# A hybrid streaming encoder step: one more gate pair as products of halves, the attention's values left in two halves, inverse sums by pairs

## The chip, the cores and the metric

The kernel runs on one core of a Trainium2 chip. The metric is device time in microseconds (us) of one execution. It is measured in several runs, and their median counts. A profile of one execution by the hardware profiler gives busy times, waits and the order in time; its span is the time from the first to the last instruction that the profiler saw.

## What is computed

One layer of an encoder step for a prompt of 1024 frames and a batch entry of 64 new frames (`sample`, with a cache of 128), together T = 1088 rows, in float32. Cut to what matters:

```python
xn = rms_norm(x, g_pre)
z = xn @ w_in                       # 1024 -> 8208 columns
xa, ga, q, k, v, gb, fl, ma, mb = jnp.split(z, ...)
ua, conv_new = causal_conv(xa, conv_hist, conv_w, conv_b)
ya, h_new = rg_lru(ua, h0, ...)     # gated recurrence over time
ya = ya * jax.nn.silu(ga)
logf = jax.nn.log_sigmoid(fl + b_f)
yb = fox_prompt(q, k, v, logf)      # causal softmax attention, 16 heads of 64;
                                    # logits + cum(logf)[query] - cum(logf)[key]
yb = yb.reshape(B, L, W_B) * jax.nn.silu(gb)
u = jnp.einsum('bsnw,nwd->bsnd', jnp.stack([ya, yb], axis=2), w_branch)
gates = jax.nn.sigmoid(jnp.stack([ma, mb], axis=2))
mix = jnp.sum(gates * u, axis=2) @ w_o
h = x + rms_norm(mix, g_post)
ple = jax.nn.sigmoid(h @ w_ple_gate) * (pe @ w_ple_proj)
return h + rms_norm(ple, g_ple), (k, v, logf, h_new, conv_new)
```

## The kernel before, in words

Everything stands transposed: 128 channels on the partitions, the rows of x along the free axis. A float32 product is made of three matmuls of halves: each operand is split into a rounded high half (`xh`, `wh`, by a copy on ScalarE, `copy_act` L89) and the rest as the low half (`xl`, `wl`, a subtraction on VectorE, `sub` L92), and high x high, low x high and high x low are added in PSUM.

The stages in order of time are:

- 0 to 145 us: x is normalised and turned; the projections v and forget gates, and two plain gate panels.
- 145 to 433 us, **the quads**: k, q and some of the other projections are made as *products of halves* (`seven`, L899). Two panels of 128 columns and two halves of the inputs form a 2 x 2 product that is made of seven products of sums instead of eight. A pair of panels takes 7 x 24 = 168 matmuls of 272 columns in place of 144 of 364 or 360. VectorE, ScalarE and GpSimd form the sums and add up the results. There are 13 such pairs; `MORE = 3` (L37) of them are gate pairs taken from the back of the deque `gates`, whose last entries are those of C_GB, the gate of branch B.
- 433 to 845 us, **the attention**: 64 units (16 heads x 4 blocks `q2` of 256 queries), plus 8 steps for pairs of heads of the sample. A unit is made of steps on TensorE: logits `s` (`scores`, L1203), turning the powers `t` (`turn`, L1228), and the product with v (`values`, L1255). Between them TensorE works at **filler** steps: plain gate panels in steps of three matmuls (`filler`, L1097), which need nothing of the attention. A planner in the kernel's own code (L1447 to L1490) sets the order: it books times of each engine and takes an attention step when its inputs will have been ready for `MARGIN(ahead_by)` ns, else a filler step. `ahead_by` says how many filler steps were used up beyond an even share of the attention so far; the margin falls from 600 ns by 60 per step, to no less than −300 (L50). What filler is left runs behind the last attention step.
- 845 to 1043 us: branch A's convolution, gates and recurrence.
- 1043 to 1111 us, **the panels of branch A**: `ya` times its half of w_branch, times sigmoid of the gate ma, written to `d_mix` (`evac_a`, L1862, one GpSimd DMA for each chunk of 364 or 360 columns). At the same time the inputs of branch B are read back: `branch_in` (L1819) loads a row block k of `d_y` and `d_gb`, `branch_b` (L1830) multiplies it by silu(gb), and `branch_out` splits it into `ybh` and `ybl`. Row blocks 0 and 1 are early ones with rooms of their own (`EARLY`, L1847), and blocks 2 to 7 use two buffers `yb_in` in turn.
- 1111 to 1207 us: the panels of branch B; then the output product, the normalisations and the embedding.

In the attention, a unit's softmax (`softmax`, L1187) takes for each half `par` of its 256 queries: exponentials with their sum `sm` on ScalarE (L1191), the inverse of the sum on GpSimd (as a power of −1, L1193), and the scaling of the powers by it on GpSimd (L1194). The value product leaves a bank `pv` of 128 partitions, whose lower 64 hold the product with v's high half and the upper 64 that with its low half. ScalarE copies the upper half to `lo`, VectorE adds the lower half to it (`y`, 64 x 256, L1293), and GpSimd issues the DMA of y to `d_y` (L1297). The deque `v_free` has two rooms for `pv`; a room is free again when the addition is done (L1295).

Of the kernel before, what the change touches and what calls it, by code (L numbers as in the profile page):

```python
# [8 lines left out]
F32 = mybir.dt.float32  # L9
# [5 lines left out]
P = 128  # L15
# [18 lines left out]
CW = HT // 2  # L34
PLAIN = 2

MORE = 3  # L37
W_SC = 1092
GC = 364

HOP_PE, HOP = 250.0, 90.0
D_MAX, D_LO, D_Y, D_YS = (240.0, 1.035), (130.0, 1.1), 420.0, 230.0
A_EXP, A_HI, A_LO, A_ST, A_W = (450.0, 0.85), (150.0, 0.88), 380.0, 470.0, 1060.0
G_NORM, G_INV = (260.0, 0.84), 220.0
G_DMA = 860.0
D_W = 1240.0

# [4 lines left out]


AHEAD = 4000
WAKE = 36
GA_EARLY = (1, 3, 5)
LN1P = [1.0 / 15, 1.0 / 13, 1.0 / 11, 1.0 / 9, 1.0 / 7, 1.0 / 5, 1.0 / 3]
# [16 lines left out]
def hybrid_step(tc, a, o):  # L74
# [24 lines left out]
    d_cq = dram.tile([2, NH, DEC], F32, name="d_cq")  # L99
    d_ma = dram.tile([KT, P, T], F32, name="d_ma")  # L100
    d_mb = dram.tile([KT, P, T], F32, name="d_mb")
    d_y = dram.tile([NP, P, T], F32, name="d_y")
    d_gb = dram.tile([KT, P, T], F32, name="d_gb")
    d_ga = dram.tile([KT, P, T], F32, name="d_ga")
    d_x = [dram.tile([P, T], F32, name=f"d_x{k}") for k in range(2)]
# [950 lines left out]
    def per(cost, n):  # L1056
        return cost[0] + cost[1] * n
# [117 lines left out]
        at = book("G", smp_at[p], 490.0, lambda: pool.tensor_copy(vs[:, :, 0, :], v_smp[:, :, :]))  # L1175
        t["vs_at"] = book("G", at, 740.0, lambda: sub(pool, vs[:, :, 1, :], v_smp[:, :, :], f(vs[:, :, 0, :])))

    def tiny2(name):
        return p2.tile([P, 1], F32, name=name, tag=name, bufs=12 if name == "nm" else 8)[:, :]

    def lowest(s, w, out, m, least=-NEG):

# [1 line left out]
        return nm, book("D", now[0] + HOP_PE, per(D_MAX, w), lambda: dve.tensor_tensor_reduce(  # L1184
            out=out, in0=s[:, :w], in1=m, scale=-1.0, scalar=least, op0=ALU.add, op1=ALU.min, accum_out=nm))

    def softmax(at, nm, n, pr):  # L1187


        sm = tiny2("sm")  # L1190
        at = book("A", at, per(A_EXP, n), lambda: act.activation(  # L1191
            out=pr[:, :n], in_=pr[:, :n], func=AF.Exp, scale=-1.0, bias=nm, accum_out=sm))
        at = book("G", at, G_INV, lambda: pool.tensor_tensor(out=sm, in0=sm, in1=warm[:, :], op=ALU.pow))  # L1193
        return book("G", at, per(G_NORM, n), lambda: pool.tensor_scalar(  # L1194
            out=pr[:, :n], in0=pr[:, :n], scalar1=sm, scalar2=1.0, op0=ALU.mult, op1=ALU.mult))

    def width(q2, par):
        n = 256 * q2 + (par + 1) * P
# [4 lines left out]
    def scores(x, i, pr):  # L1203

        h, q2 = units[x]
        t = heads[h]
        half, par = divmod(i, 2)
        n, w = width(q2, par)
        q0 = (2 * q2 + par) * P
        c = slice(half * w, (half + 1) * w)  # L1210
        s = p2s.tile([P, 512], F32, name="s", tag="s")
        pe.matmul(s[:, :w], t["q1"][:, q0:q0 + P], t["k1"][:, c], start=True, stop=False)  # L1212
        pe.matmul(s[:, :w], t["q2"][:HD + 4, q0:q0 + P], t["k2"][:HD + 4, c], start=False, stop=True)  # L1213
        spent(logits_ns(w))
        nm, at = lowest(s, w, pr[:, c], mask[:, SEQ - n + c.start:SEQ - n + c.stop],
                        nm_first.pop((x, par)) if half else -NEG)
        if c.stop < n:
            nm_first[x, par] = nm
            return at, at
        return at, softmax(at, nm, n, pr)  # L1220

    turned, turned_by = {}, {}
    n_diag = [0]
# [27 lines left out]
        return book("D", at, per(D_LO, n), lambda: sub(dve, tl[:, :n], tp[:, :n], f(th[:, :n])))  # L1251

    pvs = {}
    lo_free = [0.0]
    def values(u, g, h, q2):  # L1255
        vv = heads_v[h]
        if g == 0:
            pvs[u] = pv_half()
        pv = pvs[u]
        th, tl = turned.pop((u, g))  # L1260
        high = turned_by.pop((u, g))
        def part(j, x, **kw):
            v = vv[:, 2 * g + j, :, :].rearrange("p s d -> p (s d)")
            if g < q2:
                return pe.matmul(pv[:, :256], v, x[:, j * 256:(j + 1) * 256], **kw)  # L1265
            c0 = P if j else 0
            return pe.matmul(pv[:, c0:256], v, x[:, :P] if j else x[:, P:3 * P], **kw)  # L1267

        def high_part(j, stop=False):
            tc.declare_no_dep(part(j, th, start=False, stop=stop).ins, high.ins, reason="ordered through the low part")  # L1270

        if g < q2:
            for j in range(2):
                part(j, tl, start=(g == 0 and j == 0), stop=False)
                high_part(j)
            spent(480.0)
            return
        if q2 == 0:
            part(0, tl, start=True, stop=False)
            part(1, tl, start=False, stop=False)  # L1280
            high_part(1)
        else:
            part(1, tl, start=False, stop=False)
            high_part(1)
            part(0, tl, start=False, stop=False)
        high_part(0, True)
        spent(460.0)
        lo = p2.tile([HD, 256], F32, name="lo", tag="lo", bufs=1)
        y = p2.tile([HD, 256], F32, name="y", tag="y", bufs=3)

        dst = d_y[h // 2][(h % 2) * HD:(h % 2 + 1) * HD, q2 * 256:(q2 + 1) * 256]
        at = book("A", max(now[0] + HOP_PE, lo_free[0]), A_LO, lambda: copy_act(lo[:, :], pv[HD:, :256]))
        at = book("D", at, D_Y, lambda: dve.tensor_tensor(out=y[:, :], in0=pv[:HD, :256], in1=lo[:, :], op=ALU.add))  # L1293
        v_free.popleft()
        v_free.append(at)  # L1295
        lo_free[0] = at
        book("G", at, G_DMA, lambda: pool.dma_start(dst, y[:, :]))  # L1297


# [10 lines left out]
    def sample_scores(p):  # L1310
# [3 lines left out]
        pe.matmul(s[:, :LS], cs_q[:, :], cs_k[:, :], start=False, stop=True)  # L1314
        spent(440.0)
        nm, at = lowest(s, LS, prs_s[:, :LS], mask_s[:, :])
        return at, softmax(at, nm, LS, prs_s)

    def sample_turn(p):
        t = smp[p]  # L1320
# [9 lines left out]
    def sample_values(p):  # L1330
        t = smp.pop(p)
        pv = pv_half()
        for i in range(2):
            pe.matmul(pv[:, :], t["vs"][:, i, 0, :], t["pt"][:, i, :, :].rearrange("p s n -> p (s n)"),
                      start=(i == 0), stop=False)
            pe.matmul(pv[:, :P], t["vs"][:, i, 1, :], t["pt"][:, i, 0, :], start=False, stop=(i == 1))
        spent(458.0)
        ys = p2.tile([P, DEC], F32, name="ys", tag="ys", bufs=1)
        ats = []
        for j in range(2):  # L1340
            js, ks = slice(j * HD, (j + 1) * HD), slice(P + j * HD, P + (j + 1) * HD)
            ats.append(book("A", now[0] + HOP_PE, per(A_HI, HD), lambda js=js, ks=ks: copy_act(ys[js, :], pv[js, ks])))
        for j, at in enumerate(ats):
            js = slice(j * HD, (j + 1) * HD)
            at = book("D", at, D_YS, lambda js=js: dve.tensor_tensor(out=ys[js, :], in0=pv[js, js], in1=ys[js, :],
                                                                     op=ALU.add))
        book("D", at, 0.0, lambda: sp.dma_start(d_y[p][:, SEQ:], ys[:, :]))
        v_free.popleft()
        v_free.append(at)

# [19 lines left out]
    due = {}  # L1372
    s_free = deque([0.0, 0.0, 0.0])
    t_free = deque([0.0, 0.0])
    v_free = deque([0.0, 0.0])
    prs = {}
    seen = {"t": 0, "v": 0}
    last_t = {u: ("t", u, q2) for u, (h, q2) in enumerate(units)}
# [62 lines left out]
            t_free.append(due[step])  # L1441
        done.add(step)

    pool.memset(warm[:, :], -1.0)
    booking = tc.manual_schedule(engines={act.engine, dve.engine, pool.engine})
    booking.__enter__()
    load_head(0)  # L1447
# [16 lines left out]
    own = 0.0  # L1464
    filled = 0
    n_fill = 3 * KT * (1 + sum(e[0][0] == "r" for e in ahead) + sum(len(g[1]) for g in gates))
    head_start = n_fill
    while s_q or t_q or v_q:
        catch_up()
        times = [(i, ready(q[0])) for i, q in enumerate((s_q, t_q, v_q)) if q]  # L1470
        times = [(i, at) for i, at in times if at is not None]
        ahead_by = filled - head_start - (n_fill - head_start) * own / own_total
        best = next((i for i, at in times if at + MARGIN(ahead_by) <= now[0]), None)
        if best is None:
            at, first_ = min((at, i) for i, at in times) if times else (now[0] + 1e9, None)
# [6 lines left out]
        step = (s_q, t_q, v_q)[best].popleft()  # L1482
        own += own_time(step)
        if step == ("v", 0, 0):
            head_start = filled - n_fill * own / own_total
        go(step)
    while next(fill, False):
        catch_up()
# [328 lines left out]
        return ybpool.tile([P, T], dt, name=name, tag=f"yb{i}{k}")  # L1817

    def branch_in(k, t, z):  # L1819
        sp.dma_start(t[:, :], d_y[k])  # L1820
        sp.dma_start(z[:, :], d_gb[k])
        return t, z

# [574 lines left out]
```

## Time and profile before

| | |
|---|---|
| median of three runs | 1430.43 us (1429.32 to 1431.48) |
| the profiled execution | 1429.49 us |
| its span in the profile | 1427.5 us |
| its granted TensorE clock | 0.998 |
| instructions, all engines | 25022 |
| bytes moved by DMA | 201.20 MB, mean 141 GB/s |

In the profile PE is TensorE (matmuls), PEld its weight loads, which overlap with them, DVE is VectorE, ACT is ScalarE, POOL is GpSimd and SP the engine that issues most DMAs; a q behind the name means its queue. A row of a group gives the line, the engine, the operation and its tiles with their shapes (out<-in), the count, busy time, mean ns of one, and the idle time before them with what ended it. A DMA has two times: that of its issue on the engine and that from the issue to the landing.

### The profile page before, as it was taken

The numbers are of one execution on the slowest core, as the hardware profiler recorded it, in microseconds if no ns is written. First come the engines' busy times: TensorE is split into PE (matmuls) and PEld (weight loads), VectorE is DVE, ScalarE is ACT, GpSimd is POOL, SyncE is SP. The second block draws the span as 40 slices with busy tenths as digits, with TensorE's granted clock in tenths as the row PEclk, the third lists the DMA queues.
The fourth block names the chain that finished last, engine by engine and source line by source line (L and its number), as shares of the span: only waits on it lengthen the run. The fifth ranks groups of instructions, "written<-read, shape, count | busy, mean of one in ns | idle before, by whom it ended". The sixth has DMA issues, their size and how long they took to land.

```text
span 1427.5 us, 25022 instructions
## 1 busy us (share of the span) xinstructions
PE 1410.8 (99%) x9217; PEld 1358.0 (95%) x9217; DVE 899.4 (63%) x1638; ACT 720.5 (50%) x1339; POOL 436.5 (31%) x652
## 2 busy tenths in 40 slices
PE   9999999999999999999999999999999999999997
PEld 8999999999999999999999999999999999888887
DVE  5564766564432666666666656898767474777654
ACT  5423544442222666666666657777544232565443
POOL 0012322233204777768776841221011000000001
PEclk9999999999999999999999999999999999999999
DMA  6667556765247764556566545564467774224211
GB/s 225 214 133 107 150 155 193 162 180 141 85 122 194 182 130 131 137 110 151 123 150 131 84 101 106 83 101 84 165 211 264 252 237 136 113 74 150 78 48 45
DMA packets 138919, 201.20 MB, mean 141 GB/s; under 512 B 24372, under 2 KB 98844, under 8 KB 137772
## 3 DMA queue, kind: packets, MB, share of 16 engines
q1 hardware_dynamic: 119436, 158.96, 44.2%
q0 software_dynamic: 8160, 23.25, 5.9%
q10 hardware_dynamic: 11200, 17.38, 3.4%
q8 instruction: 73, 1.20, 0.3%
q14 instruction: 50, 0.41, 0.1%
HBM read 131.60 MB, written 66.36 MB: 139 GB/s over the span
## 4 chain that ended last, share of the span: by engine, by line
PE 82%; DVE 6%; DMA 5%; ACT 3%; issue 3%; POOL 1%; SPq 0%; DVEq 0%; ACTq 0%; POOLq 0%
PE quad L844 17%; PE acc L179 11%; PE acc L181 11%; PE acc L180 11%; PE q L2042 5%; PE tp L1244 4%; PE pv L1265 3%; PE s L1213 2%; PE s L1212 2%; PE pv L1267 2%; PE vacc L179 1%; PE vacc L180 1%; PE vacc L181 1%; DMA w_raw<-in_w_in 1%; PE vacc L500 1%
## 5 line engine op out<-in xcount | busy, mean ns | idle before, releaser
L179 PE MATMUL acc<-xh,wh 128*128 128x364 f32 x720 | 237.6, 330 | 0.2 <-ACT st L90 0.2
L181 PE MATMUL acc<-xh,wl 128*128 128x364 f32 x720 | 235.8, 328 | 0.0
L180 PE MATMUL acc<-xl,wh 128*128 128x364 f32 x720 | 235.8, 327 | 0.0
L179 PEld LDWEIGHTS acc<-xh,wh 128*128 128x128 f32 x720 | 135.4, 188 | 1.2 <-ACT st L90 0.5
L180 PEld LDWEIGHTS acc<-xl,wh 128*128 128x128 f32 x720 | 135.3, 188 | 0.8
L181 PEld LDWEIGHTS acc<-xh,wl 128*128 128x128 f32 x720 | 135.1, 188 | 0.0
L90 ACT ACTIVATE wh<-w_raw 128x1024 fp32r<-128x1024 f32 (+1 forms) x66 | 63.4, 962 | 86.4 <-PE quad L844 34.4
L93 DVE TENSOR_TENSOR wl<-w_raw,wh 128x1024 fp32r<-128x1024 f32 (+1 forms) x55 | 62.5, 1138 | 67.6 <-ACT wh L90 47.0
L1193 POOL TENSOR_TENSOR sm<-sm,warm 128x1 f32<-128x1 f32 x136 | 79.2, 582 | 57.0 <-ACT pb L1191 21.8
L93 DVE TENSOR_TENSOR tl<-tp,th 128x512 fp32r<-128x512 f32 x96 | 65.6, 687 | 38.7 <-ACT th L90 37.9
L844 PE MATMUL quad<-xh,wh 128*128 128x272 f32 x416 | 87.4, 291 | 1.8 <-ACT p__3330 L90 1.8
L844 PE MATMUL quad<-xl,wh 128*128 128x272 f32 x416 | 86.1, 288 | 0.0
L844 PE MATMUL quad<-xh,wl 128*128 128x272 f32 x416 | 86.0, 288 | 0.0
L1191 ACT ACTIVATE pb<-pb,nm 128x896 f32<-128x896 f32 (+1 forms) x64 | 63.3, 989 | 24.0 <-DVE nm L1184 21.3
L90 ACT ACTIVATE th<-tp 128x512 fp32r<-128x512 f32 x96 | 56.4, 592 | 31.0 <-PE tp L1244 30.3
L2338 POOL TENSOR_TENSOR junk<-ple,g_ple 128x256 f32<-128x256 f32 x4 | 3.8, 956 | 213.2 <-DVE ple L2295 213.2
L1212 PE MATMUL s<-k,q 128*128 128x128 f32 (+2 forms) x192 | 67.5, 353 | 0.0
L844 PEld LDWEIGHTS quad<-xh,wh 128*128 128x128 f32 x416 | 65.3, 188 | 2.3 <-ACT p__3330 L90 2.0
L1213 PE MATMUL s<-k,q 68*128 68x128 f32 (+2 forms) x192 | 65.3, 344 | 0.5 <-issue 0.5
L844 PEld LDWEIGHTS quad<-xh,wl 128*128 128x128 f32 x416 | 65.5, 188 | 0.0
L844 PEld LDWEIGHTS quad<-xl,wh 128*128 128x128 f32 x416 | 65.4, 188 | 0.0
L1194 POOL TENSOR_SCALAR pb<-pb,sm 128x896 f32<-128x896 f32 (+1 forms) x64 | 61.5, 962 | 6.2
(744 smaller groups left out, 4230.4 us busy)
## 6 DMA issues: line engine op xcount, KB each, us to landing
w_raw<-in_w_in SPq DMA_DIRECT2D x56, 256.0 KB
q<-d_q SPq DMA_DIRECT2D x48, 256.0 KB
k<-d_k SPq DMA_DIRECT2D x48, 256.0 KB
w_raw<-in_w_in SPq DMA_DIRECT2D x64, 128.0 KB
w_raw<-in_w_branch SPq DMA_DIRECT2D x32, 256.0 KB
wl<-w_raw POOLq DMA_DIRECT2D x11, 512.0 KB, 4.5
wraw<-in_w_in SPq DMA_DIRECT2D x20, 256.0 KB
d_k<-oh ACTq DMA_DIRECT2D x16, 272.0 KB
```

Source lines behind the costliest of these rows:

```text
L90: return act.activation(out=out, in_=in_, func=AF.Copy, scale=scale)
L93: return eng.tensor_tensor(out=out, in0=in0, in1=in1, op=ALU.subtract)
L179: pe.matmul(out, ah, bh, start=start, stop=False)
L180: pe.matmul(out, ah, bl, start=False, stop=False)
L181: pe.matmul(out, al, bh, start=False, stop=stop)
L844: pe.matmul(acc[:, c, :CW], l[:, k, :], r[:, k, c * CW:(c + 1) * CW], start=(first and k == 0 and p == 0), stop=(k == 3 and p == 2), skip_ ...
L1191: at = book("A", at, per(A_EXP, n), lambda: act.activation(out=pr[:, :n], in_=pr[:, :n], func=AF.Exp, scale=-1.0, bias=nm, accum_out=sm))
L1193: at = book("G", at, G_INV, lambda: pool.tensor_tensor(out=sm, in0=sm, in1=warm[:, :], op=ALU.pow))
L1194: return book("G", at, per(G_NORM, n), lambda: pool.tensor_scalar(out=pr[:, :n], in0=pr[:, :n], scalar1=sm, scalar2=1.0, op0=ALU.mult, op1 ...
L1212: pe.matmul(s[:, :w], t["q1"][:, q0:q0 + P], t["k1"][:, c], start=True, stop=False)
L1213: pe.matmul(s[:, :w], t["q2"][:HD + 4, q0:q0 + P], t["k2"][:HD + 4, c], start=False, stop=True)
L2042: pe.matmul(acc, l[:, k, :], r[:, k, :], start=(first and k == 0 and i == 0), stop=(k == 3 and i == 2), skip_group_check=not first)
```

## The change

It has three parts.

1. `MORE` goes from 3 to 4: the gate pair of panels 0 and 1 of C_GB moves from filler into the quads, so the filler has 336 steps in place of 384. `TAIL = 14` of these are left out of the planner's pace (`shared_out = n_fill - TAIL`), so that the pace foresees them for the end.
2. The whole bank `pv` is copied by one ScalarE copy to `y` (128 x 256), and both halves go to DRAM: `d_y` has a second axis for them and `d_ys` holds the sample's part. The bank has one room. The addition is made when the block is read: `branch_in` loads the first halves of the two heads by SP (64 x 1024 each), the sample's part from `d_ys`, and then GpSimd issues two transfers that add the second halves to the tile on landing.
3. The sums of a unit's two halves stand in one tile of two columns, and VectorE makes both inverses by one reciprocal when the second half's exponentials are done; only then GpSimd scales both halves. The sample has one reciprocal for each pair of heads.

```diff
-MORE = 3
+MORE = 4
+TAIL = 14
-    d_y = dram.tile([NP, P, T], F32, name="d_y")
+    d_y = dram.tile([NP, 2, P, SEQ], F32, name="d_y")
+    d_ys = dram.tile([NP, P, DEC], F32, name="d_ys")
...
-    def softmax(at, nm, n, pr):
-        sm = tiny2("sm")
-        at = book("A", at, per(A_EXP, n), lambda: act.activation(
+    def powers(at, nm, n, pr, sm):
+        return book("A", at, per(A_EXP, n), lambda: act.activation(
             out=pr[:, :n], in_=pr[:, :n], func=AF.Exp, scale=-1.0, bias=nm, accum_out=sm))
-        at = book("G", at, G_INV, lambda: pool.tensor_tensor(out=sm, in0=sm, in1=warm[:, :], op=ALU.pow))
+    def inverse(at, sm, k):
+        return book("D", at, INV, lambda: dve.reciprocal(out=sm[:, :k], in_=sm[:, :k]))
+    def normal(at, n, pr, sm):
         return book("G", at, per(G_NORM, n), lambda: pool.tensor_scalar(
             out=pr[:, :n], in0=pr[:, :n], scalar1=sm, scalar2=1.0, op0=ALU.mult, op1=ALU.mult))
+    sums = {}
...
-        return at, softmax(at, nm, n, pr)
+        if par == 0:
+            sm = tiny2("sm", 2)
+            sums[x] = sm, powers(at, nm, n, pr, sm[:, :1]), pr, n
+            return at, at
+        sm, first, pr0, n0 = sums.pop(x)
+        done_ = inverse(max(first, powers(at, nm, n, pr, sm[:, 1:])), sm, 2)
+        return at, normal(normal(done_, n0, pr0, sm[:, :1]), n, pr, sm[:, 1:])
...
-        lo = p2.tile([HD, 256], F32, name="lo", tag="lo", bufs=1)
-        y = p2.tile([HD, 256], F32, name="y", tag="y", bufs=3)
-        dst = d_y[h // 2][(h % 2) * HD:(h % 2 + 1) * HD, q2 * 256:(q2 + 1) * 256]
-        at = book("A", max(now[0] + HOP_PE, lo_free[0]), A_LO, lambda: copy_act(lo[:, :], pv[HD:, :256]))
-        at = book("D", at, D_Y, lambda: dve.tensor_tensor(out=y[:, :], in0=pv[:HD, :256], in1=lo[:, :], op=ALU.add))
+        y = p2.tile([P, 256], F32, name="y", tag="y", bufs=3)
+        dst = d_y[h // 2, h % 2][:, q2 * 256:(q2 + 1) * 256]
+        at = book("A", now[0] + HOP_PE, A_Y, lambda: copy_act(y[:, :], pv[:, :256]))
         v_free.popleft()
         v_free.append(at)
...
-    v_free = deque([0.0, 0.0])
+    v_free = deque([0.0])
...
-    head_start = n_fill
+    shared_out = n_fill - TAIL
+    head_start = shared_out
-        ahead_by = filled - head_start - (n_fill - head_start) * own / own_total
+        ahead_by = filled - head_start - (shared_out - head_start) * own / own_total
-            head_start = filled - n_fill * own / own_total
+            head_start = filled - shared_out * own / own_total
...
     def branch_in(k, t, z):
-        sp.dma_start(t[:, :], d_y[k])
+        for j in range(2):
+            sp.dma_start(t[j * HD:(j + 1) * HD, :SEQ], d_y[k, j][:HD, :])
+        sp.dma_start(t[:, SEQ:], d_ys[k])
+        for j in range(2):
+            pool.dma_start(t[j * HD:(j + 1) * HD, :SEQ], d_y[k, j][HD:, :], accum_op=ALU.add)
         sp.dma_start(z[:, :], d_gb[k])
         return t, z
```

How the order of the instructions moves is shown at three places. First GpSimd near the end of the attention, before: `sm` is the inverse of a sum (the power), `pm` and `pb` are the scaled powers, `d_y` a value block, and `d_gb` a filler panel's chunk on its way to DRAM.

```order
L1193 TENSOR_TENSOR sm<-sm,warm 128x1
L1194 TENSOR_SCALAR pm<-pm,sm 128x384
L1297 DMA d_y<-y 64x256
L1124 DMA d_gb<-st 128x360
L1193 TENSOR_TENSOR sm<-sm,warm 128x1
L1194 TENSOR_SCALAR pb<-pb,sm 128x640
L1193 TENSOR_TENSOR sm<-sm,warm 128x1
L1194 TENSOR_SCALAR pm<-pm,sm 128x512
```

And the same place of GpSimd in the changed kernel:

```order
L1126 DMA d_mb<-st 128x364
L1198 TENSOR_SCALAR pm<-pm,sm 128x384
L1198 TENSOR_SCALAR pm<-pm,sm 128x512
L1304 DMA d_y<-y 128x256
L1198 TENSOR_SCALAR pb<-pb,sm 128x640
L1198 TENSOR_SCALAR pb<-pb,sm 128x768
L1304 DMA d_y<-y 128x256
```

The powers have gone from the queue, the scalings of a unit's two halves stand next to each other, the value blocks have 128 partitions, and the last filler is of `d_mb`, since all of C_GB's panels from 0 to 7 are quads now.

The second place is GpSimd in the panels of branch A, before; there are only the chunks of `d_mix` behind the last copies of branch A (`fin`, the final states).

```order
L1639 COPY fin<-e_e 128x1
L1640 COPY fin<-e_e 128x1
L1865 DMA d_mix<-st_a 128x364 x2
L1865 DMA d_mix<-st_a 128x360
L1865 DMA d_mix<-st_a 128x364 x2
```

In the changed kernel GpSimd's queue has there, from the last chunk ahead of block 2 on:

```order
L1875 DMA d_mix<-st_a 128x360
L1875 DMA d_mix<-st_a 128x364
L1830 DMA yb_in<-d_y 64x1024 x2
L1875 DMA d_mix<-st_a 128x364
L1875 DMA d_mix<-st_a 128x360
L1830 DMA yb_in<-d_y 64x1024
L1875 DMA d_mix<-st_a 128x364
L1830 DMA yb_in<-d_y 64x1024
L1875 DMA d_mix<-st_a 128x364
```

The adding transfers of a block (two of 64 x 1024) stand between the chunks of `d_mix`; each waits for its plain load, and the chunks behind it wait with it.

The third place is VectorE in the same stage, before, around block 2: the multiplications of `yb_in`, the split `ybl`, a weight split `wl` and the evictions `st_a`.

```order
L1864 TENSOR_TENSOR st_a<-acc,gate 128x364 x2
L1837 TENSOR_TENSOR yb_in<-yb_in,gb_in 128x1088
L1826 TENSOR_TENSOR yb_in<-yb_in,gb_s 128x1088
L1864 TENSOR_TENSOR st_a<-acc,gate 128x360
L93 TENSOR_TENSOR ybl_12980<-yb_in,ybh_12979 128x1088
L93 TENSOR_TENSOR wl<-w_raw,wh 128x1024
```

And in the changed kernel:

```order
L1874 TENSOR_TENSOR st_a<-acc,gate 128x364 x2
L1847 TENSOR_TENSOR yb_in<-yb_in,gb_in 128x1088
L1874 TENSOR_TENSOR st_a<-acc,gate 128x360
L1836 TENSOR_TENSOR yb_in<-yb_in,gb_s 128x1088
L94 TENSOR_TENSOR wl<-w_raw,wh 128x1024
L1874 TENSOR_TENSOR st_a<-acc,gate 128x364
L94 TENSOR_TENSOR ybl_12777<-yb_in,ybh_12776 128x1088
```

The same instructions stand there in another sequence: an eviction and the weight split come ahead of the block's second multiplication and its split.

More of the change, by code (lines that the diff above doesn't have):

```diff
@@ L41 @@
 HOP_PE, HOP = 250.0, 90.0
-D_MAX, D_LO, D_Y, D_YS = (240.0, 1.035), (130.0, 1.1), 420.0, 230.0
-A_EXP, A_HI, A_LO, A_ST, A_W = (450.0, 0.85), (150.0, 0.88), 380.0, 470.0, 1060.0
-G_NORM, G_INV = (260.0, 0.84), 220.0
+D_MAX, INV, D_LO, D_YS = (240.0, 1.035), 165.0, (130.0, 1.1), 230.0
+A_EXP, A_HI, A_Y, A_ST, A_W = (450.0, 0.85), (150.0, 0.88), 380.0, 470.0, 1060.0
+G_NORM = (260.0, 0.84)
 G_DMA = 860.0
@@ L1176, in load_sample, with tiny2 @@
         t["vs_at"] = book("G", at, 740.0, lambda: sub(pool, vs[:, :, 1, :], v_smp[:, :, :], f(vs[:, :, 0, :])))
-    def tiny2(name):
-        return p2.tile([P, 1], F32, name=name, tag=name, bufs=12 if name == "nm" else 8)[:, :]
+    def tiny2(name, n=1):
+        return p2.tile([P, n], F32, name=name, tag=name, bufs=12 if name == "nm" else 8)[:, :]
     def lowest(s, w, out, m, least=-NEG):
@@ L1253, in hybrid_step @@
     pvs = {}
-    lo_free = [0.0]
     def values(u, g, h, q2):
@@ L1316, in sample_scores @@
         nm, at = lowest(s, LS, prs_s[:, :LS], mask_s[:, :])
-        return at, softmax(at, nm, LS, prs_s)
+        sm = tiny2("sm", 2)[:, :1]
+        return at, normal(inverse(powers(at, nm, LS, prs_s, sm), sm, 1), LS, prs_s, sm)
     def sample_turn(p):
@@ L1337, in sample_values @@
         spent(458.0)
+        yv = p2.tile([P, 256], F32, name="y", tag="y", bufs=3)
         ys = p2.tile([P, DEC], F32, name="ys", tag="ys", bufs=1)
-        ats = []
+        at = book("A", now[0] + HOP_PE, A_Y, lambda: copy_act(yv[:, :], pv[:, :256]))
+        v_free.popleft()
+        v_free.append(at)
         for j in range(2):
             js, ks = slice(j * HD, (j + 1) * HD), slice(P + j * HD, P + (j + 1) * HD)
[L1342 to L1349, printed above, removed]
+            at = book("D", at, D_YS, lambda js=js, ks=ks: dve.tensor_tensor(
+                out=ys[js, :], in0=yv[js, js], in1=yv[js, ks], op=ALU.add))
+        book("D", at, 0.0, lambda: sp.dma_start(d_ys[p], ys[:, :]))
     units = [(h, q2) for h in range(NH) for q2 in (0, 3, 1, 2)]
@@ L1442, in go @@
         done.add(step)
-    pool.memset(warm[:, :], -1.0)
     booking = tc.manual_schedule(engines={act.engine, dve.engine, pool.engine})
```

1 line of the change is left out of this document (removed).

## The prediction

> **What bounds the kernel now.** I read the page's first lines first, to see whether one engine carries the span.
>
> ```profile
> span 1427.5 us, 25022 instructions
> PE 1410.8 (99%) x9217; PEld 1358.0 (95%) x9217; DVE 899.4 (63%) x1638; ACT 720.5 (50%) x1339; POOL 436.5 (31%) x652
> ```
>
> TensorE does, and little else can: VectorE is next with 63%. So the time goes down where TensorE has less to do or waits less. The second view is the table of TensorE's waits (what it waited for, total us, times, longest).
>
> ```profile
> PE quad L844 <- ACT p__3330 L90: 1.8, 1, 1.8
> PE wake L482 <- POOL ident L127: 1.6, 1, 1.6
> PE pv L1265 <- DVE y L1293: 1.2, 4, 0.5
> PE vacc L500 <- ACT wvh L90: 1.1, 1, 1.1
> ```
>
> All waits together are a few us. Only the third belongs to instructions of this change: the value products pv wait until VectorE has emptied their bank. The third view is the busy time of each engine by stage (us of the stage, then PE, PEld, DVE, ACT, POOL, clock, DMA share, GB/s): the quads, the attention, the panels of branch A in two stretches, and a stretch of panels of branch B.
>
> ```profile
> 322.00:433.00 111.00, 111.00 (x887) 111.00 (x887) 46.49 (x59) 26.79 (x42) 25.83 (x18) 1.00 0.42 121
> 450.00:848.00 398.00, 395.91 (x2749) 385.03 (x2748) 251.83 (x671) 256.67 (x589) 281.87 (x459) 1.00 0.59 132
> 1046.00:1100.00 54.00, 53.78 (x324) 53.44 (x323) 33.54 (x42) 20.96 (x20) 11.05 (x21) 1.00 0.91 308
> 1100.00:1112.00 12.00, 12.00 (x74) 12.00 (x73) 6.64 (x8) 3.60 (x5) 1.64 (x4) 1.00 0.13 48
> 1130.00:1207.00 77.00, 77.00 (x466) 76.83 (x465) 45.28 (x101) 22.83 (x37) 0.10 (x1) 1.00 0.58 176
> ```
>
> Two things stand out. In the attention TensorE is idle for 2.1 of 398 us, and no other engine has more than 282 of them. In the panels of branch A the DMA engines, not an engine of the core, are nearly full: 0.91.
>
> **The pair that becomes products of halves.** A gate pair was 48 filler steps of three matmuls, 144 of 364 or 360 columns; as seven products of halves it is 168 matmuls of 272 columns. The chain of waits gives the price of the second kind, and the stretch 1130 to 1207 that of the first.
>
> ```profile
> 322.08 111.44 PE quad L844 x888
> ```
>
> A quad matmul: 111.44 / 888 = 125.5 ns. A panel matmul: 77.00 / 466 = 165.2 ns. So 144 x 165.2 = 23.8 us become 168 x 125.5 = 21.1 us, all on TensorE's path: **−2.7 us**. The extra sums and evictions lie beside them: the 888 matmuls are 5.3 pairs, and VectorE had 46.49 of 111 us there, some 9 per 21 us of a pair. If a pair has one more wait like the 1.8 us above, the term is −0.9; I take −2.7, since that wait is there once in the quads.
>
> On the price of a matmul the Trainium skill speaks the other way: "Perfetto Trace Analysis", Identifying the Most-Contended Engine, says that TensorE's headroom is read from the share of weight loading and not from matmul busy time. The trace disagrees as far as the edit goes: one load per matmul, 125.5 ns apart at 272 columns and 165.2 at 364. It is a rival below.
>
> **The attention: sums, scaling, values.** These rows are the lines touched, between 450 and 848 us (count, busy us, mean ns, then idle time before them and what ended it); the last is the nearest row for a reciprocal, from the whole run.
>
> ```profile
> L1193 POOL TENSOR_TENSOR sm<-sm,warm 128x1 f32<-128x1 f32 x136 | 79.2, 582 | 57.0 <-ACT pb L1191 21.8 <-DVE diag2l L93 8.1 <-DVE diag0l L93 7.6
> L1297 POOL DMA_DIRECT2D d_y<-y x64 | 37.7, 589 | 28.5 <-DVE y L1293 25.1 <-DVE nm L1184 3.1 <-issue 0.2
> L1293 DVE TENSOR_TENSOR y<-pv,lo 64x256 f32<-64x256 f32 x64 | 26.4, 412 | 32.9 <-ACT lo L90 11.9 <-PE pv L1265 7.8 <-ACT st L90 3.9
> L90 ACT ACTIVATE lo<-pv 64x256 f32<-64x256 f32 x64 | 24.4, 382 | 20.4 <-PE pv L1265 9.4 <-PE pv L1267 7.9 <-PE pv L1336 1.2
> L90 ACT ACTIVATE pts<-tps 128x256 fp32r<-128x256 f32 x8 | 3.0, 379 | 0.1
> L155 DVE RECIPROCAL r_y<-r_y 128x1 f32<-128x1 f32 (+1 forms) x18 | 2.9, 161 | 9.9 <-ACT r_y L154 9.9
> ```
>
> GpSimd loses 79.2 us of powers (281.9 to 203). VectorE gains 72 reciprocals x 161 ns = 11.6 us and loses 26.4 of adds (252 to 237). ScalarE's copy is 382 ns as lo and 379 ns for 128x256 elsewhere: no change. The d_y transfers double to 128 KB each, 64 x 64 KB = 4.2 MB more in 398 us at 132 GB/s (53 MB), at a DMA share of 0.59: hidden. None of these engines set the end, so their gain is worth nothing by itself.
>
> What is worth something is the bank: it is free after one copy (379 ns) instead of copy and add (382 + 412 ns). The four waits on y go: **−1.2 us**. Against that there is one room instead of two, and the first half's scaling now waits for the second half's exponentials. TensorE does other steps meanwhile, but there are fewer: 336 filler steps instead of 384, fourteen of them kept for the end, and the planner, running ahead of its pace, places steps up to half a us closer to their inputs. The trace has no row for this. Below, it costs nothing; above, it makes the stage's idle 2.1 us three times as long (+4.2). I take **+0.4**, a third of the old pv waits: it is nearest to those.
>
> **The values' two halves, added on the way in.** For each of the eight row blocks the branch-B input is now two plain loads, a small one and then two accumulating transfers, issued by GpSimd, that wait for the plain ones; the multiplication waits for them. Two blocks are early; six are loaded in the panels of branch A. The nearest rows are the 512 KB accumulating transfers of the weights (duration of the issue, landing), and one stretch that holds little but such a transfer.
>
> ```profile
> L297 POOL DMA_DIRECT2D wl<-w_raw x11: 853/868/917, 849.8 to 994.2; - x11
> DMA to landing us min/median/max: 4.5/4.5/4.7
> 910.20:914.80 4.60, 4.60 (x30) 4.60 (x29) 4.49 (x4) 0.59 (x2) 1.44 (x2) 1.00 0.60 114
> L1865 POOL DMA_DIRECT2D d_mix<-st_a x24: 542/542/578, 1046.9 to 1111.8; - x24
> DMA to landing us min/median/max: 2.1/5.3/7.6
> ```
>
> A block's two halves are 512 KB as well: 4.6 x 0.60 = 2.8 us of all DMA engines. Six blocks: 16.6 us. Free there are 54 x 0.09 + 12 x 0.87 = 15.3 us. The stage's transfers just fill it, so they end late in it; the d_mix row shows how far a landing stretches there, to 7.6 us. What has to be ready by when stands in the order of time (start, duration):
>
> ```profile
> 1049.30 1.17 SPq L1820 DMA_DIRECT2D yb_in<-d_y  x1
> 1050.80 0.63 SPq L1821 DMA_DIRECT2D gb_in<-d_gb  x1
> 1086.65 4.44 SPq L1820 DMA_DIRECT2D yb_in<-d_y  x2
> 1100.32 1.23 DVE L93 TENSOR_TENSOR wl<-w_raw,wh 128x1024 fp32r<-128x1024 f32 x1 [0.82 <-ACT wh L90]
> 1101.46 1.28 DVE L1837 TENSOR_TENSOR yb_in<-yb_in,gb_in 128x1088 f32<-128x1088 f32 x1
> 1105.32 1.29 DVE L93 TENSOR_TENSOR ybl<-yb_in,ybh 128x1088 fp32r<-128x1088 f32 x1 [0.73 <-ACT ybh L90]
> 1110.76 0.33 PE L179 MATMUL acc<-ybh,wh 128*128 128x364 f32 x1
> 1114.42 0.33 PE L180 MATMUL acc<-ybl,wh 128*128 128x364 f32 x1
> ```
>
> The last block's low half is done at 1105.32 + 1.29 = 1106.61, and the panel first reads it at 1114.42: a cover of 7.8 us. The last load was issued by 1091.09 and multiplied at 1101.46; taking the median landing of 5.3 off these 10.4 us, up to 5 us more may be slack: 12.8. The six blocks share two buffers, so blocks 3, 5 and 7 make a chain in which each accumulation, 4.5 to 7.6 us, comes once more; of each, 1.5 us (1049.30 to 1050.80) lie beside the gb_in load that the multiplication needs as well. That is 3 x 3.0 = 9.0 to 3 x 6.1 = 18.3 us later. Less the cover, block 7 is between 3.8 us early and 10.5 late. I take **+2.5**, a little under the middle (3.4): the larger cover is likely in part there. While VectorE waits for an accumulation, the weight split and the evictions st_a queue behind it, and TensorE waits for their banks.
>
> The page on transfers makes it less: the Trainium skill, "DMA: Bandwidth & Descriptors", Anatomy of one DMA, gives about 2.0 us and 436 GB/s for one issued by GpSimd, an estimate of 3.2 us for 512 KB. The 4.5 us above disagree and decide; by the page the chain would be 3.9 us shorter, nothing would be late, and the sum would be −3.5.
>
> **The sum.** −2.7 − 1.2 + 0.4 + 2.5 = −1.0 us. The profiled execution took 1429.49 us, 2 us around its span, so 1428.5; the median of the three runs shown, 1430.43, is 0.94 above it: **1429.4 us**. A measurement of this kernel tells about 0.2%, 2.9 us, from no change; this is within it.
>
> **Rivals.**
> - *The cover holds* (no lateness, by whichever slack): −3.5, **1426.9**. For it speaks that the chain's lower end, even with the smaller cover, is early. Against it stands the DMA share of 0.91. Chance 0.32.
> - *The accumulations are the bound* (slower): landings as long as the d_mix row's 7.6 us in each of three links, 10.5 us late: −3.5 + 10.5 = +7.0, **1437.4**. It decides from 6.4 us of lateness on. The 16.6 us of demand in 15.3 free speak for it; against it that the heavy part of the stage ends by 1100, where the share falls to 0.13. Chance 0.14.
> - *Filler runs short in the attention*: +4.2 in place of +0.4 gives +2.8, **1433.2**. For it: 12% less filler. Against it: no engine is over 71% there, and GpSimd, the fullest, loses 79 us. Chance 0.07.
> - *The load of weights is the measure*: every matmul costs its load, and a load 76.83 / 465 = 165 ns as in the panels; 24 more make +4.0 in place of −2.7, so +5.7, **1436.2**. Against it stand the two pitches. Chance 0.03. [...]
> - *The change doesn't do what it says*: the fourteen steps are used up before the end and the gained time returns as idle time; no change, **1430.4**. The order shows four filler steps behind the last pv in either program. Chance 0.02.
>
> **How the numbers follow.** The forecast has 0.42. The range reaches down to the first rival less 1.1, by which the runs shown differ from their median, 1425.8, and up to the short filler's 1433.2 with 1.4 us for the unknown wait in the new pair's products (1.8, mostly): 1434.6. Outside are the second and fourth rivals, 0.17, with the forecast's own high end inside. Faster by over 0.2% is below 1427.6: two thirds of the first rival and a fourth of the forecast, 0.32. Slower, above 1433.3: the second and fourth rivals and half of the third, 0.21. The rest, 0.47, is no change.
>
> **What would show it.** In the profile after: 24 more quad matmuls at 125 ns; no pv wait on y; in the panels of branch A a TensorE wait on st_a, ybl or a weight split of about 2.5 us in all, behind a VectorE that waits for yb_in's transfers. Landings of 3 us and no such wait make it the first rival; waits over 6 us make it the second. Idle time of over 5 us between 450 and 850 would be the third. Any wait over 2 us at another place would make the prediction wrong.

## The result and the profile after

The changed kernel took 1441.22 us, the median of four runs (1440.82 to 1443.50), against 1429.88 us before: the ratio is 1.0081, with a 95% interval of 1.0064 to 1.0099. It is slower by 11.3 us where no change was forecast, and outside the range (1425.8 to 1434.6).

The page of the profile after, its first lines:

```profile
span 1441.8 us, 25017 instructions
PE 1413.1 (98%) x9241; PEld 1362.2 (94%) x9241; DVE 892.0 (62%) x1655; ACT 711.1 (49%) x1331; POOL 372.9 (26%) x529
```

TensorE is busy for 2.3 us more than before, though the span is 14.3 us longer: the loss is waiting, and a lower TensorE clock in short stretches (last section). (This execution took 1443.5 us, the slowest of the four. 1.3 us of its surplus lie ahead of the first quad, where nothing was changed, and where the clock was at half for 3.3 us.) Its waits, in the window from 1040 to 1225 us:

```profile
PE acc L183 <- DVE wl L94: 6.9, 2, 6.0
PE held L181 <- DVE st_a L1874: 2.5, 1, 2.5
PE acc L181 <- ACT ybh L91: 1.7, 1, 1.7
PE acc L182 <- DVE ybl L94: 0.9, 1, 0.9
PE acc L181 <- ACT wh L91: 0.9, 1, 0.9
```

That is 12.9 us of waits in the panels of the branches and just ahead of them; before, the same stretch had 0.6. Some 2.5 us more are two stretches of half clock that lie there too (last section). The stages, each measured from its first matmul to the next stage's first (us):

| | before | after | difference | forecast |
|---|---|---|---|---|
| ahead of the quads | 145.2 | 146.4 | +1.3 | 0 |
| quads | 288.4 | 310.9 | +22.5 | +21.1 |
| attention, to the first recurrence gate | 425.2 | 398.9 | −26.3 | −24.6 |
| branch A, to 1050 | 192.0 | 194.2 | +2.2 | 0 |
| panels of both branches | 155.3 | 169.8 | +14.5 | +2.5 |
| the rest | 213.8 | 213.8 | 0 | 0 |

The quads and the attention come to −3.8 us together, forecast −3.5; the quads of this execution also hold 3.3 us at half clock. The next row of the quads' chain shows the matmuls of the new pair at the price that was taken, 132.52 / 1056 = 125.5 ns:

```profile
324.79 132.52 PE quad L846 x1056
```

In the attention the lines touched now read (457 to 848 us):

```profile
L1304 POOL DMA_DIRECT2D d_y<-y x64 | 36.4, 569 | 20.0 <-ACT y L91 17.5 <-ACT pts L91 2.1 <-issue 0.2
L91 ACT ACTIVATE y<-pv 128x256 f32<-128x256 f32 x72 | 27.2, 378 | 14.6 <-PE pv L1344 7.5 <-PE pv L1278 3.5 <-DMA d_y<-y 2.0
L1195 DVE RECIPROCAL sm<-sm 128x2 f32<-128x2 f32 (+1 forms) x72 | 11.8, 164 | 29.3 <-ACT pb L1191 22.4 <-ACT pm L1191 6.0
```

The copy is 378 ns, the reciprocals 11.8 us in all; both were priced rightly. So nearly the whole loss lies where the values are added. The additions, by the tile `yb_in` of the six later blocks (duration of the issue in ns, then landing):

```profile
L1830 POOL DMA_DIRECT2D yb_in<-d_y x12: 810/893/1180, 1061.5 to 1115.1; - x12
...
DMA to landing us min/median/max: 5.2/6.3/7.7
```

A transfer of 256 KB takes 5.2 to 7.7 us here, where one of 512 KB took 4.5 in branch A. The order in time shows how TensorE comes to wait. It is the start of branch B's first panel, and the column in brackets is the idle time before the instruction and what ended it:

```profile
1111.46 0.86 POOL L1830 DMA_DIRECT2D yb_in<-d_y  x1 [0.40 <-issue]
...
1114.27 0.33 PE L181 MATMUL acc<-ybh,wh 128*128 128x364 f32 x1
1114.43 0.33 PE L182 MATMUL acc<-ybl,wh 128*128 128x364 f32 x1
...
1118.31 1.29 DVE L1847 TENSOR_TENSOR yb_in<-yb_in,gb_in 128x1088 f32<-128x1088 f32 x1 [7.68 <-DMA yb_in<-d_y]
1119.51 1.22 DVE L94 TENSOR_TENSOR wl<-w_raw,wh 128x1024 fp32r<-128x1024 f32 x1
1120.65 1.28 DVE L1836 TENSOR_TENSOR yb_in<-yb_in,gb_s 128x1088 f32<-128x1088 f32 x1
1120.79 0.68 PE L183 MATMUL acc<-ybh,wl 128*128 128x364 f32 x1 [6.03 <-DVE wl L94]
```

VectorE stands idle for 7.68 us in front of a multiplication whose block is still being added: the second addition of that block is the one issued at 1111.46, and it lands at 1118.2. Behind that multiplication in VectorE's queue is the weight split wl, which needs nothing of that block, and TensorE waits 6.03 us for it. The last multiplication of a block starts at 1122.30, 20.8 us later than before.

### The profile page after: what moved, and what is told of

It is laid out like the page before. It is cut to its first block, busy times and chain, and to the rows that moved or that the text cites. A ratio compares the mean times of both kernels' runs of the same rounds, so it can differ in the third digit from the quotient of the medians.

```text
span 1441.8 us, 25017 instructions
## 1 busy us (share of the span) xinstructions
PE 1413.1 (98%) x9241; PEld 1362.2 (94%) x9241; DVE 892.0 (62%) x1655; ACT 711.1 (49%) x1331; POOL 372.9 (26%) x529
## 4 chain that ended last, share of the span: by engine, by line
PE 76%; DVE 8%; DMA 7%; issue 5%; ACT 3%; POOL 1%; SPq 0%; ACTq 0%; DVEq 0%; POOLq 0%
PE quad L846 18%; PE acc L181 9%; PE acc L183 9%; PE acc L182 9%; PE q L2052 5%; PE tp L1256 4%; PE pv L1276 3%; PE s L1219 2%; PE s L1218 2%; PE pv L1278 2%; PE vacc L181 1%; PE vacc L182 1%; PE vacc L183 1%; DMA yb_in<-d_y 1%; PE vacc L502 1%
## 5 line engine op out<-in xcount | busy, mean ns | idle before, releaser
L181 PE MATMUL acc<-xh,wh 128*128 128x364 f32 (+1 forms) x672 | 225.1, 335 | 0.8 <-ACT st L91 0.8
L183 PE MATMUL acc<-xh,wl 128*128 128x364 f32 (+1 forms) x672 | 220.1, 328 | 0.0
L182 PE MATMUL acc<-xl,wh 128*128 128x364 f32 (+1 forms) x672 | 220.1, 328 | 0.0
L181 PEld LDWEIGHTS acc<-xh,wh 128*128 128x128 f32 x672 | 126.5, 188 | 2.4 <-ACT st L91 1.4
L182 PEld LDWEIGHTS acc<-xl,wh 128*128 128x128 f32 x672 | 126.5, 188 | 1.0
L183 PEld LDWEIGHTS acc<-xh,wl 128*128 128x128 f32 x672 | 126.1, 188 | 0.0
L846 PE MATMUL quad<-xh,wh 128*128 128x272 f32 x448 | 94.8, 293 | 2.0 <-ACT p__3331 L91 2.0
L846 PE MATMUL quad<-xl,wh 128*128 128x272 f32 x448 | 93.4, 290 | 0.0
L183 PE MATMUL acc<-ybh,wl 128*128 128x364 f32 (+1 forms) x192 | 63.5, 331 | 6.0 <-DVE wl L94 6.0
L181 PE MATMUL acc<-ybh,wh 128*128 128x364 f32 (+1 forms) x192 | 63.3, 330 | 1.7 <-ACT ybh L91 1.7
```

The lines of the kernel that those rows point to most:

```text
L181: pe.matmul(out, ah, bh, start=start, stop=False)
L182: pe.matmul(out, ah, bl, start=False, stop=False)
L183: pe.matmul(out, al, bh, start=False, stop=stop)
L846: pe.matmul(acc[:, c, :CW], l[:, k, :], r[:, k, c * CW:(c + 1) * CW], start=(first and k == 0 and p == 0), stop=(k == 3 and p == 2), skip_ ...
```

## The experiments

All ratios are to the kernel before, run on the same chip. The runs came on several chips, on which the kernel before took 1429.2 to 1429.9 us, so a difference of medians between two experiments can be off by that much. Thirteen kernels ran.

**The accumulations alone.** The changed kernel with nothing but the accumulations taken out, so that the second halves of the values are missing from its result:

```diff
-        for j in range(2):
-            pool.dma_start(t[j * HD:(j + 1) * HD, :SEQ], d_y[k, j][HD:, :], accum_op=ALU.add)
```

> The changed kernel without its 16 accumulating transfers, so that the second halves of the values are left out of the result; all else stands. Theory (the loss of 14.5 us in the panels of branch A and the 2.2 us ahead of them come from the accumulations alone): no wait of TensorE over 1 us between 1045 and 1210, and the time falls from 1441.2 by 15 to 17 us to 1424.5 to 1426.5. Rival (the loads in three pieces on SP's queue and the doubled value blocks cost as well): waits on wl or ybh remain there, 1430 or more.

1424.2 us, ratio 0.9964 (0.9951 to 0.9978): 17.0 us less than the changed kernel, a little past the theory's end. The stages of branch A and of the panels are back at 192.0 and 155.3 us. The three-piece load and the doubled blocks cost nothing that can be seen; the 16 accumulations cost all of it.

**The old path of the values** (the other parts of the change stay):

```diff
-        at = book("A", now[0] + HOP_PE, A_Y, lambda: copy_act(y[:, :], pv[:, :256]))
+        at = book("A", max(now[0] + HOP_PE, lo_free[0]), A_LO, lambda: copy_act(lo[:, :], pv[HD:, :256]))
+        at = book("D", at, D_Y, lambda: dve.tensor_tensor(out=y[:, :], in0=pv[:HD, :256], in1=lo[:, :], op=ALU.add))
...
```

> The changed kernel with the old path of the values: lo copied, y added on VectorE, 64-partition blocks, two rooms, one plain load a block. The fourth gate pair, the 14 kept steps and the inverses by pairs stay. Theory (only the addition on the way in loses): panels of branch A as before, the pv waits of about 1.2 us back; 1426 to 1428. Rival (the single copy was what let the attention do with 12 per cent less filler): over 5 us idle in the attention, 1430 to 1434.

1434.39 us, ratio 1.0031 (1.0020 to 1.0042), as the rival had it, a little past its range. The panels are as before (155.3), but the attention takes 408.1 us.

**The pair alone**, on the kernel before:

```diff
-MORE = 3
+MORE = 4
+TAIL = 14
...
```

> The kernel before with only the fourth gate pair as products of halves and the 14 kept steps. Theory (the pair is worth its 2.7 us wherever the values go): 1426.5 to 1428. Rival (with the powers on GpSimd and the addition on VectorE the attention runs short of filler): waits in the attention over 4 us, 1430 to 1434.

1435.96 us, ratio 1.0038 (1.0025 to 1.0050). Again the rival, past its range: the part that was forecast to gain 2.7 us loses 6 when it is made alone. The stage by stage view of the attention, for the kernel before, this kernel, and the one without accumulations (us, then PE, PEld, DVE, ACT, POOL, clock, DMA share, GB/s):

```profile
433.52:858.72 425.20, 423.11 (x2914) 412.23 (x2912) 261.32 (x681) 263.94 (x599) 290.81 (x486) 1.00 0.60 135
```
```profile
454.50:863.00 408.50, 402.55 (x2769) 387.97 (x2768) 258.97 (x679) 258.29 (x591) 288.14 (x480) 1.00 0.59 136
```
```profile
454.60:853.30 398.70, 397.20 (x2769) 389.03 (x2768) 245.12 (x687) 249.45 (x583) 206.98 (x344) 1.00 0.62 150
```

The third column is the weight loads' busy time; what it leaves of the stage is a finer measure of TensorE's gaps than its own busy time, whose ends are modelled. It is 13.0 us before, 20.5 with the pair alone, and 9.7 with the pair and the single copy. With 2769 matmuls in either, the last two differ by 9.8 us.

**Three pairs in place of four**, with the single copy and without accumulations:

```diff
-MORE = 4
+MORE = 3
```

> The changed kernel without its accumulations (the second halves of the values are left out of the result) and with three gate pairs in place of four. It is to be held against 1424.2 with four. Theory (the pair is worth 2.7 us once the values leave by one copy, and the 6 us that it loses alone are waits for the values' additions): 1426 to 1428. Rival (the single copy itself saves the attention some 6 us or more, whatever the pair): 1421 to 1424, and the pair gains nothing.

1426.2 us, ratio 0.9973 (0.9961 to 0.9984); with four it was 0.9964 (0.9951 to 0.9978). The medians differ by 2.0 us, as the theory has it, but the intervals overlap, and the two profiled spans are 1422.4 and 1422.2 us: with four pairs the quads are 22.2 us longer there and the attention 22.3 us shorter. That the pair gains is not shown. The runs so far, by medians:

| | three pairs | four pairs |
|---|---|---|
| values added on VectorE | 1429.9 (before) | 1436.0, with reciprocals 1434.4 |
| values left by one copy | 1426.2 | 1424.2 |

The lower row is of kernels that leave the additions out. With four pairs the single copy is worth 10 to 12 us. With three the difference is some 4 us, but there the kernel with the copy has the reciprocals and the fourteen kept steps as well, and what the copy does alone was not tried.

**Bank or VectorE?** A later kernel (below, 1424.7 us) has the single copy and whole values. To it came an addition into a tile that nobody reads:

```diff
+        spare = p2.tile([HD, 256], F32, name="spare", tag="spare", bufs=1)
+        book("D", at, 420.0, lambda: dve.tensor_tensor(out=spare[:, :], in0=y[:HD, :], in1=y[:HD, :], op=ALU.add))
```

> The kernel with paced additions in DRAM (1424.7), with one more addition of 64x256 on VectorE for each value block, into a tile that nobody reads, booked as the old addition was; the bank is free after the copy as before. It puts back VectorE's 26 us without the bank's longer hold. Theory A (the old path's 9 us in the attention were the value bank, held until the addition): 1424 to 1426. Theory B (they were VectorE's load, since the maxima and the low halves of the turned powers queue behind the additions): 1430 to 1434.

1432.36 us, ratio 1.0015 (1.0005 to 1.0025): theory B. The bank is free as early as before, and most of the loss is back. The attention of this kernel:

```profile
454.40:859.00 404.60, 398.18 (x2769) 388.42 (x2767) 270.86 (x749) 247.22 (x581) 225.93 (x360) 1.00 0.66 157
```

VectorE is busy for 271 of 405 us, 67%, and some 27 us of it decide 7.7 us of the time. So the single copy relieves VectorE. That it relieves the bank as well is not excluded: the attention grew by 5.0 us here (from 399.6, below) and by 9.4 with the old path (408.1 against 398.7), and how the rest divides was not tried. Nor does the table of waits show an instruction that queues behind the additions; by which of them TensorE is held up stays open.

**The additions in DRAM.** The first trial put them behind the attention in the program, from DRAM to DRAM:

```diff
+    for k in range(NP):
+        for j in range(2):
+            pool.dma_start(d_y[k, j][:HD, :SEQ], d_y[k, j][HD:, :SEQ], accum_op=ALU.add)
...
```

> The same 16 additions of 256 KB, but from DRAM to DRAM, issued by GpSimd right behind the attention, where DMA engines were 0.54 busy; the blocks are then read by plain loads. Theory (place and chain are what cost, not the addition): 1425 to 1428 and no wait over 1 us in the panels of branch A. Rival (an accumulation costs wherever it stands, since the DMA engines or GpSimd's queue are held up for it): the weight transfers of branch A come late instead, 1433 or more.

1432.58 us, ratio 1.0013 (1.0004 to 1.0022), between the two expectations. The panels are free of the loss (155.3 us), but the scheduler moved the additions up into the attention, wherever GpSimd's queue stood, and there TensorE waited, by its table of waits:

```profile
PE tp L1256 <- POOL pm L1198: 3.4, 2, 3.3
```

The second trial gave each a place in the planned order, in the units of the next pair of heads:

```diff
+        if h >= 2 and h % 2 == 0 and q2 in (1, 2):
+            fold(h // 2 - 1, q2 - 1, lambda do: book("G", at, G_DMA, do))
...
```

> The additions again from DRAM to DRAM, but put in the attention's planned order at places where the blocks of a pair of heads have long landed (two places in the next pair's units), so that GpSimd's queue does not wait for them; only the last pair's two stand at the end. Theory (the 3.3 us wait of TensorE on pm and the 8 us longer attention of the first DRAM trial came from accumulations that stood in GpSimd's queue and waited for the blocks): attention as in the kernel without accumulations, 1424 to 1427. Rival (DRAM accumulations slow the other transfers, of q, k and the weights): 1430 or more.

1424.71 us, ratio 0.9960 (0.9946 to 0.9974): a whole kernel that is faster than before by 5.2 us and than the changed one by 16.5. The additions' rows (issue in ns, landing in us) and the attention of this kernel:

```profile
L1266 POOL DMA_DIRECT2D d_y<-d_y x16: 788/892/920, 551.5 to 845.0; - x16
...
DMA to landing us min/median/max: 4.0/5.0/15.3
```
```profile
455.88:855.50 399.62, 397.26 (x2769) 389.02 (x2768) 243.06 (x685) 247.65 (x581) 220.56 (x360) 1.00 0.67 159
```

One of them took 15.3 us to land, and nobody waited: the first reader comes over 100 us later.

**Without the fourteen kept steps**, and **with the powers back on GpSimd**, both on this kernel:

```diff
-TAIL = 14
+TAIL = 0
```

> The kernel with paced additions in DRAM (1424.7), with no filler steps kept out of the pace. Theory (the planner keeps step with its inputs either way once the values leave by one copy, so the fourteen steps are worth nothing): 1424 to 1426. Rival (they are what prevents short waits at the attention's end): idle time there, 1427 or more.

1427.84 us, ratio 0.9991 (0.9983 to 1.0000): 3.1 us more by medians, and the intervals are apart. In the profiles 2.0 us lie in the attention and 1.9 behind it, where less filler covers the first recurrence block (0.9 us wait on ul, 0.8 on uh). The kept steps are worth their place.

```diff
-        done_ = inverse(max(first, powers(at, nm, n, pr, sm[:, 1:])), sm, 2)
-        return at, normal(normal(done_, n0, pr0, sm[:, :1]), n, pr, sm[:, 1:])
+        return at, softmax(at, nm, n, pr)
...
```

> The kernel with paced additions in DRAM (1424.7), with the third part undone: inverse sums as powers on GpSimd, each half scaled on its own. Theory (GpSimd's 79 us are off the path, part 3 is worth nothing or up to the 1.6 us between the two kernels with the old value path): 1424.5 to 1426.5. Rival (with the paced additions and the powers GpSimd becomes late): tp waits on pm or pb, 1428 or more.

1425.20 us, ratio 0.9968 (0.9956 to 0.9981): no difference from 0.9960 that these runs can tell. The third part is not shown to do anything by itself.

**What makes a link of the chain long?** First more rooms: blocks 2 and 3 are loaded into rooms of blocks 5 and 6, which are free then.

```diff
+        if k < 4:
+            t, z = branch_in(k, *(row_room(8 - k, i, F32, f"in2_{i}{k}") for i in "hl"))
+        else:
-        t, z = branch_in(k, p4.tile([P, T], F32, name="yb_in"), p4.tile([P, T], F32, name="gb_in"))
+            t, z = branch_in(k, p4.tile([P, T], F32, name="yb_in"), p4.tile([P, T], F32, name="gb_in"))
```

> The changed kernel with four rooms for the branch-B inputs in place of two: blocks 2 and 3 are loaded and added in rooms of their own that are free then, so blocks 4 to 7 share the two buffers and a chain has two links in place of three. Bytes and transfers are the same. Theory (the chain of load, accumulation and multiplication through two buffers makes the 16.7 us that stand between 1441.2 and 1424.2): a link in three goes, at 5 to 7 us each and with it a further start, 1428 to 1434. Rival (the stage's DMA engines are full, so bytes decide): landings stay at 6 to 8 us and the time within 3 us of 1441.2.

1431.6 us, ratio 1.0010 (1.0001 to 1.0019): 9.6 of the 17 us come back with the same bytes, and landings that are no shorter (6.1 to 9.3 us). What remains is the same kind of wait:

```profile
PE acc L183 <- DVE wl L94: 3.5, 1, 3.5
```

Then half the bytes (the accumulation stops at 512 columns, and the rest of the second halves is left out):

```diff
-            pool.dma_start(t[j * HD:(j + 1) * HD, :SEQ], d_y[k, j][HD:, :], accum_op=ALU.add)
+            pool.dma_start(t[j * HD:(j + 1) * HD, :SEQ // 2], d_y[k, j][HD:, :SEQ // 2], accum_op=ALU.add)
```

> The changed kernel with accumulations of 512 columns in place of 1024: the other half of the second halves is left out of the result. As many transfers, links and issues, half the accumulated bytes. Theory (each link costs mostly its landing's fixed part, its issue and its place in the queue): two thirds of the 17 us stay, 1435 or more. Rival (bytes): half stays or less, 1433 or less.

1438.97 us, ratio 1.0065 (1.0051 to 1.0078): 2.2 us less by medians, with overlapping intervals, so it is not shown that the bytes are worth anything. The landings go from a median of 6.3 to 5.5 us. Between 1050 and 1110 us the DMA engines' share was 0.79 to 0.83 in stretches of 20 us, where the changed kernel had 0.89 to 1.01, and the panels of the profiled execution still took 171.9 us (169.8 in the changed kernel). So the loss doesn't need full DMA engines.

Last, GpSimd's queue, in which accumulations stand between chunks of `d_mix` that wait for VectorE:

```diff
-            pool.dma_start(d_mix[of][:, t0:t0 + n], s[:, :n])
+            act.dma_start(d_mix[of][:, t0:t0 + n], s[:, :n])
```

> The changed kernel with the chunks of d_mix issued by ScalarE in place of GpSimd, so that the accumulations stand alone in GpSimd's queue. Bytes, buffers and links are the same. Theory (an accumulation waits in GpSimd's queue behind a chunk whose st_a stands on VectorE behind the last block's multiplication, which makes one chain of all six blocks): accumulations are issued as soon as their loads land, and 4 to 9 us of the 17 go: 1432 to 1437. Rival (full DMA engines set the pace): landings grow and the time is within 2 us of 1441.2.

1441.51 us, ratio 1.0084 (1.0065 to 1.0102): nothing comes back, and my theory of the queue falls. GpSimd's timeline and the plain loads of block 3 on SyncE's queue tell why:

```profile
1059.72 1.14 SPq L1827 DMA_DIRECT2D yb_in<-d_y  x2
```
```profile
1068.38 1.75 POOL L1830 DMA_DIRECT2D yb_in<-d_y  x2 [10.06 <-DMA yb_in<-d_y]
1081.40 1.64 POOL L1830 DMA_DIRECT2D yb_in<-d_y  x2 [11.27 <-DMA yb_in<-d_y]
```
```profile
1077.61 1.29 DVE L1847 TENSOR_TENSOR yb_in<-yb_in,gb_in 128x1088 f32<-128x1088 f32 x1 [7.08 <-DMA yb_in<-d_y]
```

GpSimd now waits for the loads themselves: 8.7 us from the load's issue to the accumulations' issue, and 9.2 us from there to the multiplication. A link is load, then accumulations, then multiplication, whatever stands in the queue. The time is the rival's, and the landings grew as it said (median 6.9 us), but the half bytes speak against full DMA engines as the cause.

The same with SyncE:

```diff
-            pool.dma_start(d_mix[of][:, t0:t0 + n], s[:, :n])
+            sp.dma_start(d_mix[of][:, t0:t0 + n], s[:, :n])
```

> The same with SyncE issuing the chunks of d_mix. By the theory on GpSimd's queue the accumulations are free of the chunks here too: 1432 to 1437. But SyncE also issues the loads, and those that wait for a buffer hold up the chunks behind them: if the loads' queue matters more, 1440 or more. Rival (full DMA engines): within 2 us of 1441.2.

1449.58 us, ratio 1.0135 (1.0110 to 1.0160): the chunks hold up the loads, and the panels take 177.8 us. Between 1040 and 1130 us SyncE stood 43.9 us, in nine waits, ahead of chunks whose st_a was not done.

## Why the prediction was wrong

- **The pair's price** (−2.7 us): the two pitches stand (125.5 ns after). The quads grew by 22.5 us instead of 21.1, with 3.3 us at half clock among them; in the ten other kernels that have the pair and no such stretch there, they grew by 19.9 to 21.1. As a gain of its own the pair isn't shown: alone it loses 6 us, and with the single copy its 2.0 us are within the intervals. The rival on the load of weights priced a load at 165 ns; in the quads the prediction's own row has 111.00 / 887 = 125.1.
- **The attention** (−1.2 and +0.4): the sum with the pair came out, −3.8 against −3.5, by luck: its terms were off, and the half clock in the quads is in it. Without such a stretch the two stages came to −5.4 to −6.4 in the four other kernels with the same path of the values into DRAM and no additions there. I wrote that none of these engines set the end, "so their gain is worth nothing by itself", and priced the copy by four waits on y. The spare addition shows that some 27 us on VectorE are worth 7.7 with four pairs. The rival of the short filler was real, and its +4.2 too small: with the pair alone the attention fell by 16.7 us, 7.1 less than the 23.8 us of filler that had gone. The single copy, in the same change, paid for it.
- **The powers** at nothing: not contradicted (0.5 us, within the intervals).
- **The early blocks** at nothing: wrong by 2.2 us in this execution. VectorE waited 3.8 us for their accumulations, and TensorE then 2.5 us on st_a. With four rooms, where the early blocks are the same, that stretch took 192.4 us, so the 2.2 us vary.
- **The step that failed** is "I take +2.5": the panels and the stretch ahead cost 16.7 us in the profile, 17.0 by medians. The mechanism was the second rival's, "the accumulations are the bound", and its 10.5 us were too few as well. Two pieces of its working were off. A link was taken as 3.0 to 6.1 us more; the last multiplication came 20.8 us later, 6.9 for each of three links: a block's two accumulations follow each other on one queue and land in 5.2 to 7.7 us, behind plain loads that take their time as well. And the cover was taken from ybl's row, 7.8 to 12.8 us. The instruction that TensorE waited for was the split wl, which ended at 1101.55 before, 9.2 us ahead of the panel, and stood behind another block's multiplication: it ended 19.2 us later. I had named wl as queued there, and gave it no cover of its own.
- **Bytes or steps**: the sum of DMA time (16.6 us of demand in 15.3 free) gave a fair warning for the wrong reason. With half the bytes most of the loss stays (2.2 us less by medians, within the intervals); fewer links bring 9.6. How the remaining 7 us of the kernel with four rooms divide was not tried.
- By the page on transfers, the Trainium skill's "DMA: Bandwidth & Descriptors", Anatomy of one DMA, an estimate for 256 KB is 2.6 us. The traces of these accumulating transfers disagree: 3.8 us at the least in any of these kernels (the first trial in DRAM), and 6.3 in the middle of a stage whose DMA engines are full.

## What to carry to other kernels

An addition that moves from an engine into a load adds a whole landing to each use of the buffer; count it by the links of the buffer's chain, at the landing of a full stage, and put it where the reader is far away (5.2 us gained) instead of where the data is needed (11.3 lost). For the cover of a late instruction, look at everything that stands behind it in its engine's queue, not at its own consumer alone. An engine at 63 to 67% can still set the time of a stage that has little filler left, so the worth of taking work from it has to be tried with the filler that the new kernel will have.

## What the runs showed of the hardware

The granted TensorE clock fell after short idle times. In the changed kernel, in windows of 5 us:

```profile
1085.00:1090.00 5.00, 3.22 (x16) 2.62 (x16) 3.67 (x5) 3.17 (x3) 2.56 (x4) 0.95 0.98 272
1090.00:1095.00 5.00, 5.00 (x24) 5.00 (x23) 0.33 (x1) 1.11 (x1) 0.32 (x1) 0.71 1.01 261
...
1120.00:1125.00 5.00, 4.21 (x17) 4.21 (x18) 5.00 (x6) 2.11 (x2) 0.60 (x1) 0.63 0.15 46
```

These clocks are averages of windows that lie partly in a stretch of lower clock. Finer windows show that it was at half; the first two are the stretches ahead of the quads and in them:

```profile
14.40:17.70 3.30, 3.30 (x16) 3.16 (x16) 2.64 (x7) 1.34 (x3) 0.00 (x0) 0.50 0.51 159
290.90:294.20 3.30, 3.30 (x16) 3.30 (x16) 2.75 (x12) 0.21 (x1) 1.34 (x1) 0.50 0.58 217
1089.60:1092.90 3.30, 3.30 (x13) 3.30 (x12) 0.00 (x0) 1.11 (x1) 0.60 (x1) 0.50 1.02 210
1116.90:1123.60 6.70, 2.81 (x9) 2.81 (x10) 5.29 (x6) 1.63 (x2) 0.60 (x1) 0.50 0.54 127
```

The third came after two waits of TensorE, 0.87 us and 0.91 us, in the 2.4 us from 1086.6 on. In its 3.3 us 13 matmuls started; at full clock it would be 20. So a wait cost more than its own length: about 1.2 us more here (7 matmuls of 165 ns). The fourth began 2.1 us into the wait of 6 us and outlasted it by 2.8 us. No plain threshold comes out of these runs: the stretch in the quads stands behind a wait of 2.0 us, and a wait of 2.1 us at the same place in the kernel with the spare addition had none behind it. The Trainium skill, "TensorE: Matmul & The Clock Gate", Part 1, puts such a drop after an idle window of some 3.4 us; here 1.8 us in two pieces were enough.
